# Gates of one of three dense token tiles: indirect adding DMAs into a zeroed tensor in place of one-hot matmuls

## The chip, the cores and the metric

One of the cores of a Trainium2 chip runs the whole kernel. Its engines are TensorE (PE, matrix products), VectorE (DVE), ScalarE (ACT), GpSimd (POOL) and SyncE (SP, which only starts transfers). The metric is the device time of one execution in microseconds.

## The reference

One decoder layer on 512 tokens and 16 meta tokens: projections, differential attention and a gated linear recurrence, an output projection, and then PEER, a channel mixer that chooses experts by product keys. Only PEER is touched:

```python
q = jnp.einsum('nd,dc->nc', xb, w_query).reshape(PEER_BLOCK, PEER_HEADS, 2, PEER_QUERY_DIM // 2)
s = jnp.einsum('nhpc,hpkc->nhpk', q, subkeys).astype(jnp.float32)
sv, si = lax.top_k(s, PEER_TOPK)
cand_s = (sv[:, :, 0, :, None] + sv[:, :, 1, None, :]).reshape(PEER_BLOCK, PEER_HEADS, PEER_TOPK * PEER_TOPK)
cand_i = (si[:, :, 0, :, None] * N_KEYS + si[:, :, 1, None, :]).reshape(PEER_BLOCK, PEER_HEADS, PEER_TOPK * PEER_TOPK)
top_s, pos = lax.top_k(cand_s, PEER_TOPK)
experts = jnp.take_along_axis(cand_i, pos, axis=-1).reshape(PEER_BLOCK, PEER_HEADS * PEER_TOPK)
gates = jax.nn.softmax(top_s, axis=-1).reshape(PEER_BLOCK, PEER_HEADS * PEER_TOPK)
hid = jax.nn.gelu(jnp.einsum('nkd,nd->nk', u_table[experts], xb), approximate=False) * gates
return jnp.einsum('nk,nkd->nd', hid, v_table[experts])
```

There are 128 x 128 experts of width 1024, 8 heads and 16 experts a head: each token has 128 gates. Inside a head the 16 experts differ; two heads may name the same one, and then their gates add up.

## The kernel before

The 512 tokens are four tiles of 128. For three of them (tiles 0 to 2, the dense tiles) PEER is computed over all 16,384 experts: U in 128 blocks of 128 experts against the 384 tokens (`ps_h`, 24 matmuls of 128x128 by 128x384 a block: three products per slice, since each number is split into a high and a low part), gelu into `hr`, times a dense gate matrix, then V (`y`). For the fourth tile (`SP`, number 3) the chosen rows of U and V are gathered by 256 indirect DMAs of GpSimd, 128 rows each (`ug`, `vg`).

The dense gates are a tensor in DRAM, `g_dram`, indexed by group of 32 tokens, second key, first key and token. The dense part reads it back in slices `gsl` of 4 blocks.

The stretch in question lies between the choice of the experts (about 465 us) and the dense part (from 751 us):

- `route(tb)` (L781) turns the positions in the sorted lists into expert indices, in `pick` with steps on 128x2048 elements on VectorE, each after an expansion by ScalarE (L789). For the gathered tile it ends in `exp_idx`, for a dense tile in `pmj`, transposed by TensorE (`ptp`).
- `gates4` (L832) makes the dense gates of four tokens: two VectorE operations build one-hots `oh` (L837, L843), eight TensorE matmuls (L850, L851) multiply them into `pgt`, and ScalarE copies these into `stg` (L852). After 8 calls four DMAs (L889) store 32 tokens. There are 96 calls, 32 for each dense tile.
- Between them `run_ahead` computes the hidden values of the first 40 U blocks ahead of time (the ring, `RING` = 40), in quarters of a block, `RATE` = 0.8 quarters a call of `gates4`. `h_parts` does one block: a load `ur` from SP, the high part `uh` on ScalarE, the low part `ul` on the engine that `eng` names (here GpSimd, `G`; L107), 24 matmuls and the gelu (L698).
- The dense part (L896 on) loads `gsl` (L975) and V (`vr`, L977), splits V into `vh` and `vl`, multiplies `hr` by the slice (`hr`, L982), splits that into `wh` and `wl`, and runs the `y` matmuls; `h_parts` of block i + 40 stands behind those of block i, and the gathers of the fourth tile are spread over the blocks.

A scheduler orders the instructions of each engine from the program; on VectorE in the dense part the order is that of the code. SP starts nearly all transfers, in its own order: a transfer that waits for something holds up those behind it.

In the front (the first 70 us) SP loads the weights `wr` of the projections, 512 KB each, two to a piece, and the pieces are split on ScalarE (`wh`) and VectorE (`wl`) before TensorE uses them. `mf` are masks.

Of the kernel before, what the change touches and what calls it, by code (L numbers as in the profile page):

```python
# [8 lines left out]
F32 = mybir.dt.float32  # L9
F32R = mybir.dt.float32r  # L10
F16 = mybir.dt.float16
U32 = mybir.dt.uint32
# [30 lines left out]
GI = 4  # L43
# sums of a pair of descending lists that can be among the 16 largest:
# (first row, rows, columns) of the blocks that cover (a + 1) * (b + 1) <= 16
CBLK = [(0, 1, 16), (1, 1, 8), (2, 2, 5), (4, 4, 3), (8, 8, 1)]
NCAND = sum(n * m for _, n, m in CBLK)
RING = 40
HP = 4
RATE = 0.8  # L50
DRAIN = 0.3
W2 = 10
LAG = 2


# [5 lines left out]
def tile_kernel(  # L61
# [30 lines left out]
    h_dram = dram.tile([SEQ, D], F32, name="h_dram")  # L92
    g_dram = dram.tile([DTOK // GB, NK, NK, GB], F32, name="g_dram")

# [5 lines left out]
    def rstd(dst, ssq, n, width):  # L100
        """dst = (ssq / n + eps) ** -0.5 for [P, width] tiles."""
        G.tensor_scalar(dst, ssq, 1.0 / n, EPS, op0=OP.mult, op1=OP.add)
        G.tensor_tensor(dst, dst, nhalf[: dst.shape[0], :width], op=OP.pow)
# [9 lines left out]

    # ------------------------------------------------------------------ front
    with ExitStack() as fr:
# [10 lines left out]
        with ExitStack() as pr:  # L126
# [94 lines left out]

            # ---- HGRN2 projections
            Q, QF, KR, FF = [], [], [], []
# [30 lines left out]

            # gates' lower bound: softmax over the two rows of logits, first row
            lg = fc.tile([P, 2, NH], F32, name="lg")
# [12 lines left out]
            for pc in range(2):  # L269
                for cb in range(2):  # L270
# [15 lines left out]
                    KR.append(k)  # L286
            # lambda
            lq = fc.tile([P, 4, 64], F32, name="lq")
# [22 lines left out]
            V.tensor_copy(idb, ident)  # L311

            cosr = xp.tile([P, T], F32, name="cosr")
            sinr = xp.tile([P, T], F32, name="sinr")
# [5 lines left out]
            for pc in range(2):  # L320
                w = w_piece(2 + pc)
                for cb in range(2):
# [10 lines left out]
                    QF.append(qf)  # L333
            # ---- HGRN2: scores inside the chunks, by a tree of decays
            AT = [hg.tile([P, NTB, P], F32, name=f"at{h}") for h in range(NH)]
# [43 lines left out]

            # ---- HGRN2: states at the chunks' starts and outputs  # L380
            def keys(h):
# [51 lines left out]

            # ---- attention projections
            AQ, AK = [], []
            for which, lst, lo in ((8, AQ, NMETA), (10, AK, 0)):
                for pc in range(2):
                    w = w_piece(which + pc)
                    for cb in range(2):
                        n = T - lo  # L440
                        raw = tp.tile([P, T], F32, name="raw", tag="w2", bufs=W2)
                        segs = [(lo, T)] if n <= 512 else [(0, HALF), (HALF, T)]
                        for a, b in segs:
                            ps = proj_t(w, cb, a, b)
                            S.activation(raw[:, a - lo : b - lo], ps, AF.Copy, scale=0.125 if lo else 1.0)
                        rot = tp.tile([P, T], F32, name="rot", tag="w2", bufs=W2)
                        for g in range(4):
                            src = (g ^ 1) * 32
                            nc.sync.dma_start(rot[g * 32 : g * 32 + 32, :n], raw[src : src + 32, :n])
                        hh = pc * 2 + cb  # L450
                        V.tensor_tensor(rot[:, :n], rot[:, :n], sinr[:, lo:], op=OP.mult)
                        if lo:
                            # one query of the pair per half, zeros in the other
                            r = aqp.tile([P, 2, SEQ], F32, name=f"aq{hh}")
                            G.memset(r[64:, 0], 0.0)
                            G.memset(r[:64, 1], 0.0)
                            V.tensor_tensor(raw[:, :n], raw[:, :n], cosr[:, lo:], op=OP.mult)
                            for p2 in range(2):
                                r0 = slice(p2 * 64, p2 * 64 + 64)
                                V.tensor_tensor(r[r0, p2], raw[r0, :n], rot[r0, :n], op=OP.add)  # L460
                        else:
                            r = hp_.tile([P, T], F32, name=f"ak{hh}", tag=f"f{hh}")
                            V.tensor_tensor(r, raw, cosr, op=OP.mult)
                            V.tensor_tensor(r, r, rot, op=OP.add)
                        lst.append(r)
            # ---- attention core
            def scores(h, tb):
# [61 lines left out]

            # gate of the recurrence, times the norm's weight  # L530
            wg = {}
# [112 lines left out]

        # ------------------------------------------------------ output projection
        xbp = ctx.enter_context(tc.tile_pool(name="xbp", bufs=1, reuse_waits="tile"))
# [28 lines left out]

    # --------------------------------------------------------------- PEER
    ringp = ctx.enter_context(tc.tile_pool(name="ringp", bufs=RING, reuse_waits="tile"))
# [9 lines left out]
    def h_parts(i, eng=None, n=1):  # L687
        """gelu of block i's hidden values, in n steps; the last one appends it to the ring"""
        h_load(i, eng)
        if eng is not None and i + 1 < RING:  # L690
            h_load(i + 1, eng)
# [15 lines left out]
    with ExitStack() as rt:  # L707
# [10 lines left out]
        G.iota(io_f, pattern=[[1, P]], base=0, channel_multiplier=0, allow_small_or_imprecise_dtypes=True)  # L718
        V.tensor_copy(io16, io_f[:, :16])
        starts = rc.tile([P, 16], I16, name="starts")  # L720
        o = 0
# [52 lines left out]
        rw = rt.enter_context(tc.tile_pool(name="rg", bufs=2, reuse_waits="tile"))  # L774
        steps = (None for i in range(RING) for _ in h_parts(i, G, HP))

# [4 lines left out]
        def route(tb):  # L781
            # experts' two key indices
            idx = []

            def pick(which, sel, op, key, table, dt):
                """idx of the selected key: sum over a of op(sel, key[a]) * table[a]"""
                eq = rw.tile([P, PH * TOPK, TOPK], dt, name="eq", tag="eq", bufs=1)
# [10 lines left out]

            # first list: rank a is the last one whose candidates start at or before the position;
            # 64 * key + start comes out as a sum of the table's steps  # L800
            comb = rw.tile([P, PH, TOPK], I16, name="comb", bufs=1)
# [17 lines left out]
            if tb == SP:  # L819
                V.scalar_tensor_tensor(  # L820
                    exp_idx, idx[0].rearrange("p h k -> p (h k)"), float(NK), idx[1].rearrange("p h k -> p (h k)"),
                    op0=OP.mult, op1=OP.add,
                )
                return None
            ptp = pg.tile([P, 4, P], F32, name="ptp", tag="pg")
            for i, t in enumerate((idx[0], idx[1], gh[:, tb], TS[tb])):
# [5 lines left out]
        def gates4(pmj, t0, stg, c0):  # L832
            """dense gates of four tokens: one-hots of the first key, of it times the gate's two parts, of the second"""
            oh = rw.tile([P, 4, P, 4], F16, name="oh", bufs=3)
# [19 lines left out]
        run_ahead(16)  # L854
        # gates, in two parts of 11 bits for the dense blocks
        fl = "p t h k -> p (t h) k"
# [7 lines left out]
        V.tensor_tensor(g3, g3, mx.unsqueeze(2).to_broadcast([P, NTB * PH, TOPK]), op=OP.mult)  # L864
        V.tensor_copy(exp_g, TS[SP].rearrange("p h k -> p (h k)"))
        gh16 = rw.tile([P, ND, PH, TOPK], F16, name="gh16", bufs=1)
        gh = rw.tile([P, ND, PH, TOPK], F32, name="gh", bufs=1)
# [3 lines left out]
        V.tensor_tensor(TSA[:, :ND], TSA[:, :ND], gh, op=OP.subtract)  # L871

        run_ahead(4)
        route(SP)
        run_ahead(8)
        nxt = route(0)
        run_ahead(16)
        acc_ = 0.0
        for tb in range(ND):
            pmj = nxt  # L880
            for g0 in range(0, P, GB):
# [6 lines left out]
                for i0 in range(0, NK, 32):  # L888
                    nc.sync.dma_start(g_dram[(tb * P + g0) // GB, :, i0 : i0 + 32, :], stg[:, i0 : i0 + 32, :])  # L889
                if g0 == P // 2 - GB and tb + 1 < ND:  # L890
# [5 lines left out]

    # dense part for the first ND token blocks, gathered part for the last
    with ExitStack() as dn:
# [64 lines left out]
        for i in range(NK):  # L963
# [9 lines left out]
            if i % GI == 0:  # L973
                gsl = dp.tile([P, DTOK // GB, GI, GB], F32, name="gsl", bufs=2)
                nc.sync.dma_start(gsl, g_dram[:, :, i : i + GI, :].rearrange("g j i t -> j g i t"))  # L975
            vr_ = dp.tile([P, D], F32, name="vr", tag="vr", bufs=3)
# [94 lines left out]
```

## Time and profile before

| | |
|---|---|
| Three executions | 1656.05, 1659.43, 1655.10 us |
| Median | 1656.05 us |
| Span of the profiled execution | 1655.8 us |
| TensorE busy | 1595.0 us (96%) |
| VectorE busy | 1246.4 us (75%) |
| ScalarE busy | 672.6 us (41%) |
| GpSimd busy | 566.7 us (34%) |
| Transfers | 363.93 MB, mean 220 GB/s |

The profile comes from one execution, whose span runs from its first to its last instruction and is its own time; it lies 0.25 us under the median. Busy time is the sum of an engine's instructions; TensorE's matmuls overlap, so that the duration of one (297 ns for a `pgt` matmul) is longer than the distance to the next. The chain of waits follows what ended last back through its causes. The granted clock is TensorE's, 1.00 being full speed.

### The profile page before, as it was taken

How to read it: one execution, taken by the hardware profiler on the slowest of the kernel's cores; microseconds unless marked ns; L12 is line 12 of the kernel's file. 1: busy time of each engine (PE TensorE's matmuls, PEld its weight loads, DVE VectorE, ACT ScalarE, POOL GpSimd, SP SyncE). 2: the span in 40 equal slices, each digit the busy share in tenths (PEclk: the TensorE clock that was granted, in tenths of full speed). 3: DMA queues.
4: the chain of work that ended last, by engine and by line, in shares of the span. 5: the costliest groups of instructions: out<-in, count | busy, mean ns of one | idle time of the engine just before them, and what ended most of it. 6: DMA issues, size and time to landing. Idle time of an engine off the chain costs nothing.

```text
span 1655.8 us, 23775 instructions
## 1 busy us (share of the span) xinstructions
PE 1595.0 (96%) x8859; PEld 1427.1 (86%) x8859; DVE 1246.4 (75%) x2375; ACT 672.6 (41%) x1017; POOL 566.7 (34%) x429
## 2 busy tenths in 40 slices
PE   7999998999978889999999999999999999999997
PEld 7899986888777889898999999999999999988886
DVE  6772568568898897837877778777777777767776
ACT  5123265422245666753433333333333333323333
POOL 2000012334444223254444444444444444433221
PEclk9999999999988999999999999999999999999999
DMA  6211322322222354569999988998898999877884
GB/s 205 77 50 45 118 71 103 115 90 77 73 81 100 143 203 174 207 228 357 337 322 319 324 306 308 318 323 309 311 331 304 318 321 314 311 233 262 282 278 144
DMA packets 145635, 363.93 MB, mean 220 GB/s; under 512 B 11888, under 2 KB 61296, under 8 KB 145392
## 3 DMA queue, kind: packets, MB, share of 16 engines
q1 hardware_dynamic: 107936, 227.10, 39.4%
q0 software_dynamic: 37008, 134.27, 23.4%
q8 instruction: 69, 1.13, 0.3%
q10 hardware_dynamic: 576, 1.05, 0.2%
q14 instruction: 46, 0.38, 0.1%
HBM read 330.92 MB, written 29.36 MB: 218 GB/s over the span
## 4 chain that ended last, share of the span: by engine, by line
PE 80%; DVE 13%; ACT 2%; DMA 1%; issue 1%; POOL 1%; SPq 0%; POOLq 0%; DVEq 0%; ACTq 0%
PE y L112 10%; PE y L111 10%; PE y L110 10%; PE ps_h L112 9%; PE ps_h L110 9%; PE ps_h L111 9%; PE pgt L850 2%; DVE oh L837 2%; PE pgt L851 2%; DVE oh L843 2%; PE ps_t L110 2%; PE ps_l L342 2%; PE ps_t L112 2%; PE ps_t L111 2%; PE ps_n L110 1%; PE ps_n L111 1%
## 5 line engine op out<-in xcount | busy, mean ns | idle before, releaser
L110 PE MATMUL ps_h<-xbh,uh 128*128 128x384 f32 x1024 | 355.1, 347 | 9.1 <-ACT hr L698 9.1
L112 PE MATMUL ps_h<-xbh,ul 128*128 128x384 f32 x1024 | 348.3, 340 | 3.3 <-POOL ul L107 3.3
L111 PE MATMUL ps_h<-xbl,uh 128*128 128x384 f32 x1024 | 347.6, 339 | 0.0
L110 PE MATMUL y<-vh,wh 128*128 128x512 f32 x768 | 299.0, 389 | 3.2 <-ACT wh L106 3.0
L112 PE MATMUL y<-vh,wl 128*128 128x512 f32 x768 | 300.9, 392 | 0.0
L111 PE MATMUL y<-vl,wh 128*128 128x512 f32 x768 | 300.4, 391 | 0.0
L922 POOL DMA_INDIRECT vg<-in_v_dram,exp_idx x128 | 185.3, 1448 | 277.8 <-DVE acc L928 210.6
L908 POOL DMA_INDIRECT ug<-in_u_dram,exp_idx x128 | 177.5, 1387 | 215.7 <-DVE jk L912 151.2
L107 DVE TENSOR_TENSOR vl<-vr,vh 128x1024 fp32r<-128x1024 f32 x128 | 156.8, 1225 | 123.0 <-ACT vh L106 121.1
L106 ACT ACTIVATE vh<-vr 128x1024 fp32r<-128x1024 f32 x128 | 136.0, 1062 | 266.2 <-issue 215.2
L106 ACT ACTIVATE uh<-ur 128x1024 fp32r<-128x1024 f32 x144 | 152.7, 1062 | 158.8 <-issue 69.4
L107 POOL TENSOR_TENSOR ul<-ur,uh 128x1024 fp32r<-128x1024 f32 x57 | 151.2, 2658 | 191.9 <-ACT uh L106 191.9
L110 PEld LDWEIGHTS ps_h<-xbh,uh 128*128 128x128 f32 x1024 | 197.2, 193 | 13.7 <-ACT hr L698 10.1
L111 PEld LDWEIGHTS ps_h<-xbl,uh 128*128 128x128 f32 x1024 | 196.3, 192 | 3.5
L112 PEld LDWEIGHTS ps_h<-xbh,ul 128*128 128x128 f32 x1024 | 195.3, 191 | 3.6 <-POOL ul L107 3.6
L110 PEld LDWEIGHTS y<-vh,wh 128*128 128x128 f32 x768 | 144.2, 188 | 31.9 <-ACT wh L106 4.2
L112 PEld LDWEIGHTS y<-vh,wl 128*128 128x128 f32 x768 | 144.1, 188 | 31.1 <-DVE wl L107 0.9
L111 PEld LDWEIGHTS y<-vl,wh 128*128 128x128 f32 x768 | 144.1, 188 | 28.3
L106 ACT ACTIVATE wh<-hr 128x384 fp32r<-128x384 f32 x128 | 67.2, 525 | 246.4 <-DVE hr L982 241.7
L928 DVE SCALAR_TENSOR_TENSOR acc<-vg,hid,acc 128x1024 f32<-128x1024 f32 x127 | 162.7, 1281 | 3.3 <-DMA vg<-in_v_dram,exp_idx 1.4
L912 DVE SCALAR_TENSOR_TENSOR jk<-ug,xbn 128x1024 f32<-128x1024 f32 x128 | 156.4, 1222 | 8.9 <-DMA ug<-in_u_dram,exp_idx 6.5
L107 DVE TENSOR_TENSOR wl<-hr,wh 128x384 fp32r<-128x384 f32 x128 | 71.5, 559 | 83.7 <-ACT wh L106 83.1
(268 smaller groups left out, 2716.5 us busy)
## 6 DMA issues: line engine op xcount, KB each, us to landing
ur<-in_uT_dram SPq DMA_DIRECT2D x128, 512.0 KB
vr<-in_v_dram SPq DMA_DIRECT2D x128, 512.0 KB
g_dram<-stg SPq DMA_DIRECT2D x48, 512.0 KB
gsl<-g_dram SPq DMA_DIRECT2D x32, 768.0 KB
wr<-in_w_in_dram SPq DMA_DIRECT2D x26, 512.0 KB
ur<-in_wq_dram SPq DMA_DIRECT2D x16, 512.0 KB
wor<-in_w_out_dram SPq DMA_DIRECT2D x8, 512.0 KB
xr<-in_xT_dram SPq DMA_DIRECT2D x8, 264.0 KB
```

The costliest lines, as they stand in the source:

```text
L106: S.activation(hi, src, AF.Copy)
L107: (eng or V).tensor_tensor(lo, src, hi.bitcast(F32), op=OP.subtract)
L110: PE.matmul(ps, ah, bh, start=first, stop=False)
L111: PE.matmul(ps, ah, bl, start=False, stop=False)
L112: PE.matmul(ps, al, bh, start=False, stop=last)
L342: PE.matmul(ps[:, c, :], KR[h][:, cs], rhs[:, c * P : c * P + P], start=True, stop=True)
L837: V.tensor_tensor(oh[:, :2], io128.unsqueeze(1).to_broadcast([P, 2, P, 4]), pmj[:, :2, tq4].unsqueeze(2).to_broadcast([P, 2, P, 4]), op=OP ...
L843: V.tensor_tensor(oh[:, 2:], oh[:, 0:1].to_broadcast([P, 2, P, 4]), pmj[:, 2:, tq4].unsqueeze(2).to_broadcast([P, 2, P, 4]), op=OP.mult,)
L908: G.indirect_dma_start(out=ug, out_offset=None, in_=u, in_offset=bass.IndirectOffsetOnAxis(ap=exp_idx[:, k : k + 1], axis=0))
L912: V.scalar_tensor_tensor(jk, ug, 1.0, xbn_, op0=OP.mult, op1=OP.mult, accum_out=hid[:, k : k + 1])
L922: G.indirect_dma_start(out=vg, out_offset=None, in_=v, in_offset=bass.IndirectOffsetOnAxis(ap=exp_idx[:, k : k + 1], axis=0))
L928: V.scalar_tensor_tensor(acc, vg, hid[:, k : k + 1], acc, op0=OP.mult, op1=OP.add)
```

## The change

Tile 0's gates are no longer made by `gates4`. A tile `zero` is cleared by GpSimd in the front, and SP writes it over the whole of `g_dram[0]` in four transfers of 2 MB. When `route(0)` has the indices, two VectorE operations compute the place of each gate in `g_dram[0]`, `sc_idx`, from the two keys, the group and the token (`base_i`). `scatter` then issues 128 indirect DMAs from GpSimd, one for each head and rank; each adds 128 gates of 4 bytes, one per token, into `g_dram[0]`. The DMAs of one head are independent of each other; each DMA of a head waits for all 16 of the head before.

`g_dram` becomes three tensors, one per dense tile, and the load of a slice three transfers; the first of them waits for the last head. The loop over `gates4` runs over tiles 1 and 2 only, with `RATE` 1.5. The routes come in the order 0, `SP`, 1 (then 2 inside the loop) where they came in the order `SP`, 0 (then 1 and 2). The low parts `ul` of the look-ahead blocks are made by VectorE.

```diff
-RATE = 0.8
+RATE = 1.5
...
-    g_dram = dram.tile([DTOK // GB, NK, NK, GB], F32, name="g_dram")
+    g_dram = [dram.tile([P // GB, NK, NK, GB], F32, name=f"g_dram{t}") for t in range(ND)]
...
+            zero = tp.tile([P, 16, GB], F32, name="zero", tag="w2", bufs=W2)
+            G.memset(zero, 0.0)
+            for g in range(P // GB):
+                nc.sync.dma_start(
+                    g_dram[0][g].rearrange("j (a b) t -> j a b t", b=16),
+                    zero.unsqueeze(1).to_broadcast([P, NK // 16, 16, GB]),
+                )
...
-        if eng is not None and i + 1 < RING:
+        if n > 1 and i + 1 < RING:
             h_load(i + 1, eng)
...
+        base_i = rc.tile([P, 1], F32, name="base_i")
+        for g in range(P // GB):
+            G.iota(
+                base_i[g * GB : g * GB + GB], pattern=[[0, 1]], base=g * NK * NK * GB, channel_multiplier=1,
+                allow_small_or_imprecise_dtypes=True,
+            )
...
-        steps = (None for i in range(RING) for _ in h_parts(i, G, HP))
+        steps = (None for i in range(RING) for _ in h_parts(i, None, HP))
...
+            if tb == 0:
+                off = rc.tile([P, PH, TOPK], F32, name="off")
+                sc_idx = rc.tile([P, PH, TOPK], U32, name="sc_idx")
+                V.tensor_scalar(off, idx[0], float(GB), base_i[:, 0:1], op0=OP.mult, op1=OP.add)
+                V.scalar_tensor_tensor(sc_idx, idx[1], float(NK * GB), off, op0=OP.mult, op1=OP.add)
+                return sc_idx
...
+        sc_g = rc.tile([P, PH, TOPK], F32, name="sc_g")
+        V.tensor_scalar(sc_g, TS[0], GS, None, op0=OP.mult)
...
+        def scatter(sc_idx):
+
+            flat = g_dram[0].rearrange("g j i t -> (g j i t)").unsqueeze(1)
+            before = []
+            for h in range(PH):
+                now = []
+                for k in range(TOPK):
+                    ins = G.indirect_dma_start(
+                        out=flat, out_offset=bass.IndirectOffsetOnAxis(ap=sc_idx[:, h, k : k + 1], axis=0),
+                        in_=sc_g[:, h, k : k + 1], in_offset=None, compute_op=OP.add,
+                    ).ins
+                    tc.declare_no_dep(ins, group=f"head{h}", reason="one head's experts differ")
+                    tc.add_to_no_dep_group(f"head{h}", ins)
+                    for b in before:
+                        tc.add_manual_dep(ins, b.name, SYNC, reason="the head before may have the same expert")
+                    now.append(ins)
+                before = now
+            return before
+
         run_ahead(4)
+        scattered = scatter(route(0))
+        run_ahead(8)
         route(SP)
         run_ahead(8)
-        nxt = route(0)
+        nxt = route(1)
         run_ahead(16)
         acc_ = 0.0
-        for tb in range(ND):
+        for tb in range(1, ND):
...
-                    nc.sync.dma_start(g_dram[(tb * P + g0) // GB, :, i0 : i0 + 32, :], stg[:, i0 : i0 + 32, :])
+                    nc.sync.dma_start(g_dram[tb][g0 // GB, :, i0 : i0 + 32, :], stg[:, i0 : i0 + 32, :])
...
-                nc.sync.dma_start(gsl, g_dram[:, :, i : i + GI, :].rearrange("g j i t -> j g i t"))
+                for t in range(ND):
+                    gs_ = nc.sync.dma_start(
+                        gsl[:, t * (P // GB) : (t + 1) * (P // GB)],
+                        g_dram[t][:, :, i : i + GI, :].rearrange("g j i t -> j g i t"),
+                    ).ins
+                    if t == 0:
+                        for b in scattered:
+                            tc.add_manual_dep(gs_, b.name, SYNC, reason="the last head's gates")
```

GpSimd's order behind the candidates' sums (`cand`), before: 35 low parts, then the gathers `ug`.

```order
L763 TENSOR_TENSOR cand<-sva 128x4x10
L763 TENSOR_TENSOR cand<-sva 128x4x12
L763 TENSOR_TENSOR cand<-sva 128x4x8
L763 TENSOR_TENSOR cand<-sva 128x4x16
L107 TENSOR_TENSOR ul<-ur,uh 128x1024 x35
L908 DMA ug<-in_u_dram,exp_idx 128x1024 x2
```

And now: the 128 scatters stand there, and one low part is left (of the block behind the ring); the gathers come behind them.

```order
L779 TENSOR_TENSOR cand<-sva 128x4x12
L779 TENSOR_TENSOR cand<-sva 128x4x8
L779 TENSOR_TENSOR cand<-sva 128x4x16
L904 DMA g_dram_61<-sc_g,sc_idx 2097152x1 x128
L108 TENSOR_TENSOR ul<-ur,uh 128x1024
L953 DMA ug<-in_u_dram,exp_idx 128x1024 x32
```

The low parts have left GpSimd, and the scatter stands between the sums and the fourth tile's gathers.

SP's order at the start of the dense part, before (`g_dram<-stg` the gates' stores, `ur` U blocks, `gsl` the first slice, `vr` V blocks):

```order
L889 DMA g_dram<-stg 128x1024 x4
L655 DMA ur<-in_uT_dram 128x1024 x2
L889 DMA g_dram<-stg 128x1024 x4
L655 DMA ur<-in_uT_dram 128x1024 x2
L975 DMA gsl<-g_dram 128x12x128
L977 DMA vr<-in_v_dram 128x1024 x3
L655 DMA ur<-in_uT_dram 128x1024
L977 DMA vr<-in_v_dram 128x1024
```

And now:

```order
L934 DMA g_dram_63<-stg 128x1024 x4
L664 DMA ur<-in_uT_dram 128x1024 x3
L934 DMA g_dram_63<-stg 128x1024 x4
L1021 DMA gsl<-g_dram_61 128x4x128
L1021 DMA gsl<-g_dram_62 128x4x128
L1021 DMA gsl<-g_dram_63 128x4x128
L1029 DMA vr<-in_v_dram 128x1024 x3
```

The slice is three transfers, of which that from `g_dram_61` (tile 0's) waits for the scatter; the first three V blocks follow behind it, as before.

VectorE's order ahead of the first one-hot `oh`, before (`eq`, `sif`, `ix` are steps of `route(0)`; the last `eq`, `starts` is the first of `route(1)`):

```order
L790 TENSOR_TENSOR eq<-eq,io_3431 128x2048
L792 TENSOR_TENSOR eq<-eq,sif 128x2048
L794 TENSOR_TENSOR eq<-eq 128x128x8
L817 CAST sif<-si_3456 128x128
L794 TENSOR_TENSOR eq<-eq 128x128x4
L794 TENSOR_TENSOR eq<-eq 128x128x2
L796 TENSOR_TENSOR ix_5046<-eq 128x128
L790 TENSOR_TENSOR eq<-eq,starts 128x2048
L837 TENSOR_TENSOR oh<-io_3432,pmj 128x1024 x2
L843 TENSOR_TENSOR oh<-oh,pmj 128x1024 x2
L837 TENSOR_TENSOR oh<-io_3432,pmj 128x1024
```

And now (steps of `route(1)`, the third one, and then the first of `route(2)`):

```order
L108 TENSOR_TENSOR ul<-ur,uh 128x1024
L806 TENSOR_TENSOR eq<-eq,io_3439 128x2048
L808 TENSOR_TENSOR eq<-eq,sif 128x2048
L108 TENSOR_TENSOR ul<-ur,uh 128x1024
L810 TENSOR_TENSOR eq<-eq 128x128x8
L833 CAST sif<-si_3470 128x128
L810 TENSOR_TENSOR eq<-eq 128x128x4
L810 TENSOR_TENSOR eq<-eq 128x128x2
L812 TENSOR_TENSOR ix_5291<-eq 128x128
L806 TENSOR_TENSOR eq<-eq,starts 128x2048
L859 TENSOR_TENSOR oh<-io_3440,pmj 128x1024 x2
L865 TENSOR_TENSOR oh<-oh,pmj 128x1024 x2
```

The first one-hot stands behind a third route, and low parts `ul` stand between the routes' steps: 18 of them ahead of the first one-hot, where there were none. TensorE has 409 `ps_h` matmuls ahead of the first `pgt` matmul where it had 264, and 986 ahead of the first `y` matmul where it had 960.

## Rows read from the trace of the kernel before

**Rows 1.** Windows, all engines: busy us (count); then granted clock, DMA share, GB/s.

```profile
core 0: us, PE busy (x) PEld busy (x) DVE busy (x) ACT busy (x) POOL busy (x), PEclk, DMA share, GB/s
...
680.00:737.00 57.00, 56.23 (x380) 52.43 (x380) 36.59 (x45) 35.90 (x40) 20.14 (x9) 1.00 0.58 213
737.00:751.00 14.00, 11.35 (x66) 11.02 (x64) 1.69 (x2) 3.86 (x6) 7.41 (x5) 1.00 1.01 386
751.00:800.00 49.00, 48.62 (x244) 43.97 (x245) 42.84 (x63) 19.14 (x28) 24.61 (x17) 1.00 0.96 348
800.00:900.00 100.00, 100.00 (x508) 91.08 (x507) 80.05 (x99) 36.43 (x49) 45.30 (x34) 1.00 0.91 321
```

**Rows 2.** Chain of waits, 720 to 760: start, length, what.

```profile
737.37 13.41 DMA vr<-in_v_dram
...
751.38 0.50 PE y L110
```

**Rows 3.** Timeline of SP's queue: start, length, line, transfer.

```profile
41.95 54.72 SPq L141 DMA_DIRECT2D wr<-in_w_in_dram  x8
...
735.62 0.38 SPq L975 DMA_DIRECT2D gsl<-g_dram  x1
```

**Rows 4.** Timeline of VectorE in the routes: start, length; idle before, who ended it.

```profile
470.81 3.28 DVE L792 TENSOR_TENSOR eq<-eq,step 128x2048 int16<-128x2048 int16 x1
...
482.91 1.22 DVE L792 TENSOR_TENSOR eq<-eq,sif 128x2048 f16<-128x2048 f16 x1
...
491.21 0.29 DVE L820 SCALAR_TENSOR_TENSOR exp_idx<-ixa,ix 128x128 uint32<-128x128 f32 x1
...
508.96 0.43 DVE L796 TENSOR_TENSOR ix<-eq 128x128 f32<-128x128 f16 x1
...
513.04 1.28 DVE L837 TENSOR_TENSOR oh<-io,pmj 128x1024 f16<-128x1024 f16 x2
```

**Rows 5.** Timeline of TensorE, 468 to 482; 18 matmuls from 470.90 to 476.75.

```profile
470.90 0.69 PE L110 MATMUL ps_h<-xbh,uh 128*128 128x384 f32 x1 [5.34 <-ACT hr L698]
471.38 0.53 PE L111 MATMUL ps_h<-xbl,uh 128*128 128x384 f32 x1
471.70 0.53 PE L112 MATMUL ps_h<-xbh,ul 128*128 128x384 f32 x1
...
476.75 0.33 PE L110 MATMUL ps_h<-xbh,uh 128*128 128x384 f32 x1
476.92 0.34 PE L111 MATMUL ps_h<-xbl,uh 128*128 128x384 f32 x1
```

**Rows 6.** Windows of `pgt` alone: TensorE, ScalarE busy; then clock, DMA.

```profile
680.00:725.00 45.00, 25.76 (x192) 26.13 (x24) 1.00 0.54 198
```

**Rows 7.** Windows of `ps_h` alone: TensorE, its weight loads, ScalarE.

```profile
725.00:740.00 15.00, 15.00 (x88) 15.00 (x87) 1.42 (x3) 1.00 0.80 280
```

**Rows 8.** Tile `oh`: durations in ns as min/median/max.

```profile
L837 DVE TENSOR_TENSOR oh<-io,pmj x96: 673/686/2823, 513.0 to 719.1; 128x1024 f16<-128x1024 f16 x96
```

**Rows 9.** Line 107 (low parts): min/median/max ns.

```profile
L107 DVE TENSOR_TENSOR ul<-ur,uh x87: 1210/1218/1221, 758.3 to 1466.0; 128x1024 fp32r<-128x1024 f32 x87
...
L107 POOL TENSOR_TENSOR ul<-ur,uh x57: 2343/2412/5164, 312.8 to 742.5; 128x1024 fp32r<-128x1024 f32 x57
```

**Rows 10.** Timeline of GpSimd, gathers of 735 to 775 and from 1500.

```profile
740.28 0.95 POOL L908 DMA_INDIRECT ug<-in_u_dram,exp_idx  x1 [0.16 <-issue]
741.54 0.94 POOL L908 DMA_INDIRECT ug<-in_u_dram,exp_idx  x1 [0.30 <-issue]
...
1500.80 1.74 POOL L922 DMA_INDIRECT vg<-in_v_dram,exp_idx  x1 [2.34 <-DVE acc L928]
```

**Rows 11.** Timeline of VectorE at 1500.

```profile
1500.49 1.23 DVE L107 TENSOR_TENSOR vl<-vr,vh 128x1024 fp32r<-128x1024 f32 x1
```

**Rows 12.** Line 908, the gathers of U: min/median/max ns.

```profile
L908 POOL DMA_INDIRECT ug<-in_u_dram,exp_idx x128: 934/1516/1865, 735.3 to 1440.4; - x128
```

**Rows 13.** Tile `rot`: idle time before its users (us, times), by releaser.

```profile
  DMA rot<-raw: 17.0, 8
```

**Rows 14.** Timeline of ScalarE in the front.

```profile
48.00 2.01 ACT L106 ACTIVATE wh<-wr 128x1024 fp32r<-128x1024 f32 x2 [4.02 <-PE ps_t L111]
```

**Rows 15.** Timeline of TensorE in the front.

```profile
63.61 0.36 PE L110 MATMUL ps_n<-wh,xh 128*128 128x256 f32 x1
```

More of the change, by code (lines that the diff above doesn't have):

```diff
@@ L53 @@
 LAG = 2
+SYNC = mybir.DependencyInfo(mybir.DependencyClass.Sync, mybir.DependencyReason.DATA)
 def row_bcast(ap, n, parts=P):
```

## The prediction, made before the changed kernel ran

> **What bounds the kernel now.** I read the windows table first. TensorE is full nearly everywhere; from 680 on it is the longest bar in every stretch but one [rows 1]. That one, 737 to 751, is the seam this change works on: the last gates are stored, TensorE runs out of look-ahead blocks, and the dense part has not begun. The chain of waits says why [rows 2]: the first y matmul at 751.38 waits for a V block that was 13.41 us on its way, asked for by SP only after the gates' first slice, `gsl`, at 735.62 [rows 3]: 15.8 us from slice to first y. So whatever lets SP issue that slice earlier moves everything after it, until TensorE is what is late. After the seam TensorE has no slack (100.00 of 100 us, 800 to 900 [rows 1]), so a time gained or lost at the first y arrives at the end undiminished. That is the frame of the sum: when does the first y start, and how much look-ahead is then already done.
>
> Ahead of the gates the bound is another: VectorE turns sums into expert indices (route), and its first one-hot starts at 513.04 [rows 4], while TensorE stands still in parts and runs at the lower of its two clock levels, half pace (1.2 for 2.4 GHz): after a wait of 5.34 us at 470.90 the matmuls come 0.32 us apart, from 476.92 on 0.18 [rows 5]. From 517 to the seam the gates' work is a mix: three TensorE jobs (look-ahead, gates, a few transposes) one behind the other.
>
> **What leaves TensorE.** Tile 0's 32 groups of gates go: 256 `pgt` matmuls. In a stretch with 192 of them TensorE counted 25.76 us [rows 6], 134 ns each, so 34 us leave. The look-ahead stays: 88 `ps_h` matmuls took 15.00 us [rows 7], 0.170 each. The VectorE one-hots (64 of 0.68 us [rows 8]), copies and stores of that tile go too; they lie beside TensorE's work and I count them at nothing.
>
> **What moves on VectorE before the first one-hot.** Three routes now precede it (tile 0, the gathered tile, tile 1) where two did. One route takes from the end of the gathered tile's (491.21) to the end of tile 0's (508.96), 17.8 us [rows 4]; without the two steps that were held up beside GpSimd, 14. Eighteen `ul` parts come to VectorE ahead of the first one-hot at 1.22 us each [rows 9]: +22. Against that GpSimd's `ul` work vanishes, and with it the collisions: the same multiplication took 3.28 us beside it and 1.22 alone [rows 4]; six such steps lie in 467 to 513, 2.1 each: -12.5. Sum: 513.0 + 14 + 22 - 12.5 = 536.5; the first gate matmul some 4 us behind, as before: 540.5. In that time TensorE can run 409 look-ahead matmuls where it had 264 (the program's order), 25 us more in 24 us more, so its stand-still there stays as it was.
>
> **When TensorE is ready for the dense part.** From 540.5: 577 look-ahead matmuls (986 less 409) at 0.170 = 98, and 64 groups of 8 gate matmuls at 0.134 = 69; 707.5. The same count for before (696 and 768 from 517.1) gives 738, and the last look-ahead ended about 748 (11.35 of 14 us busy [rows 1]); half of that slack, since two thirds of the groups are left and nothing slows the one-hots: 712. VectorE's load there (128 one-hots at 0.68, 22 `ul` at 1.22, one route) is 130 us of 170, so it does not bind.
>
> **When the scatter ends.** This is the new wait, and the largest unknown. SP's first `gsl` waits for the eighth head; in the order SP has V's loads behind that wait, so V's split and the first y wait with it. The indices: before, the first route ended at 491.21 [rows 4]; now four collisions less (-8.4), ten `ul` on VectorE up to there (+12.2): 495. Then eight heads one behind the other, each 15 issues and the last one's flight. No row shows an accumulating indirect DMA; the nearest are the gathers, which GpSimd issues the same way. Free, one starts 1.26 us after the last (740.28 to 741.54); one that meets a VectorE operation with two inputs in SBUF waits until it ends: 1.74 at 1500.80 beside a subtraction that ran from 1500.49 [rows 10, 11]. The median over the dense part is 1.52 [rows 12], which with 0.30 between makes 1.82. In the scatter's time VectorE is busy some three quarters with operations of 0.68 and 1.22 us, so that an issue waits 0.75 x 0.42 = 0.32: 1.58, between the ends 1.26 and 1.82. The flight: small rope transfers held VectorE up 17.0 us in 8 times, 2.1 each [rows 13], a floor; the ceiling is the 13.41 us of rows 2, in a crowd that the scatter doesn't have. I take 4.5, twice the floor, since an addition reads before it writes; that is a choice. A head: 15 x 1.58 + 4.5 = 28.2; eight: 226; the end at 721. Ends: 1.26 and 2.1 give 663, 1.82 and 8 give 778.
>
> On the issue cost the Trainium skill speaks otherwise ("SBUF — State Buffer", Who interferes with whom): a tensor_tensor takes only the shared pair's read side, and descriptor generation is inferred to need the write side, so the two should pass each other. Rows 10 and 11 show a subtraction of just that kind with a gather behind it; I go by the row. By the rule the issues would stay at 1.26 (first rival). On the flight it speaks against the change ("DMA: Bandwidth & Descriptors", Anatomy of one DMA): a fixed cost of about 2.0 us, mostly the receipt of the write, heaviest in HBM; no row shows it for 4-byte additions. By 2.0 the head would be 25.7 and the scatter's end 701.
>
> **The first y.** With 721 as the later of the two (TensorE 712), SP then issues three slices and V. Before it took 15.8 us with a look-ahead U block and four 512 KB gathers in the queue at 386 GB/s [rows 1]; now the U block is there already, and less is ahead of V: I take 11, bounds 8 and 16. The first y at 732 against 751.4: -19.4. TensorE stood 20 us, so some 18 matmuls run at half pace [rows 5]: +2.6. By then 26 look-ahead matmuls more are done than before (986 against 960): -4.4.
>
> **The front.** GpSimd clears a tile, SP sends four 2 MB zero writes ahead of the weights that it issues at 41.95 [rows 3]. At 386 GB/s 8.4 MB take 22 us, from about 32 to 54, at 300 to 60. The two weight splits at 48.00 [rows 14] would then find their data at 55 to 62, and TensorE wants them at 63.61 [rows 15]; a split and its low part are 2 to 3.5 us. So 0 to 4 us: I take 2, and up to 9 if the transfers behind it pile up.
>
> **Sum:** 1655.8 - 19.4 + 2.6 - 4.4 + 2 = 1636.6; the profiled span lies 0.25 under the median of 1656.05, so about 1637.
>
> **Rivals.** (A) The scatter is not late. If a head takes under 25.8 us (issues at 1.26 to 1.4), it ends by 701 and TensorE alone sets the first y, at 713: -38.4 - 4.4 + 2 = 1615. At the free pace of rows 10 a head is 15 x 1.26 + 4.5 = 23.4 and the end 682. For it: most of VectorE's gate work is of short operations, and no row shows one of 0.68 us holding an issue up. Against: the 1.8 us of rows 10 and 12. The Trainium skill's rule on the shared pair, above, would bring just this case. 0.25. (B) The scatter is slower than what it replaces. GpSimd's issues behind VectorE, or additions with a long flight: a head over 30.6 us puts the end past 740 and the first y past 751, and from there each us per head costs eight. At the dense part's 1.82 and 4.5 a head is 31.8, the end 749, the first y 760, and 1655.8 + 8.8 + 2.6 + 2 - 4.4 = 1665; with a flight of 8, 35.3, 777 and 1692. For it: the median of rows 12 and 128 issues that can't overlap across heads; nothing in the trace bounds an addition's flight. 0.30 beyond +0.3%. (C) The zeroing stops the front: 9 us in place of 2 makes 1644, inside the range. (D) The freed TensorE time is not on the path because VectorE's longer preamble eats it: if the first gate came at 560, TensorE would be ready at 732, still with the scatter; it would change nothing by itself.
>
> **How the numbers follow.** Chances: the forecast's mechanism (a scatter that ends between 701 and 736, time 1615 to 1651) 0.35; A 0.25; about even (end 736 to 746; within 0.3%, which is what a measurement of this kernel can tell from none) 0.10; B 0.30. Faster 0.60, same 0.10, slower 0.30. The range leaves out a tenth on each side: 1612 (A without a front delay) to 1690 (B with a flight of 8). Without B the likeliest one's own range is 1615 to 1651.
>
> **What would show it.** Starts of the first scatter (495), of each head (28 apart) and of the last; the wait on SP before the first `gsl`, and who ends it; first one-hot at 536; TensorE's idle time ahead of the first y, some 20 us; the first y near 732; the half-pace matmuls behind it; the weight split of 48.00 at 55 to 62. The forecast is wrong if a head takes under 25 or over 31 us, or if TensorE, not SP, is the last to arrive.

## The result and the profile after

The changed kernel takes 1692.4 us (median of 4 runs, 1689.8 to 1697.0) against 1655.6 of the kernel before: 1.0225 times as long, with a 95% interval of 1.0205 to 1.0246. Forecast were 1637 us, and a range of 1612 to 1690. The profiled execution spans 1695.2 us. From its page (the third line is TensorE's granted clock in 40 slices, the last the queue of GpSimd's transfers):

```profile
span 1695.2 us, 23411 instructions
...
PE 1559.5 (92%) x8599; PEld 1397.2 (82%) x8599; DVE 1197.9 (71%) x2354; ACT 642.1 (38%) x984; POOL 683.7 (40%) x522
...
PEclk9999999999899999656999999999999999999999
...
q0 software_dynamic: 55440, 134.34, 25.4%
```

In slices 17 to 19 the granted clock falls to 0.5 and 0.6. The windows around them (columns as in [rows 1]):

```profile
640.00:680.00 40.00, 40.00 (x271) 37.32 (x270) 28.34 (x38) 25.02 (x29) 28.64 (x18) 1.00 0.66 185
680.00:692.00 12.00, 11.27 (x73) 10.43 (x71) 0.10 (x1) 6.92 (x9) 10.17 (x7) 1.00 0.24 2
692.00:770.00 78.00, 0.00 (x0) 0.00 (x0) 0.00 (x0) 0.22 (x1) 61.72 (x41) 0.51 0.20 0
770.00:790.00 20.00, 7.25 (x24) 6.93 (x24) 1.70 (x2) 3.37 (x4) 7.16 (x6) 0.59 0.82 289
790.00:800.00 10.00, 9.62 (x30) 7.71 (x31) 8.68 (x14) 2.41 (x4) 4.34 (x3) 0.67 1.05 404
800.00:900.00 100.00, 100.00 (x507) 90.89 (x505) 84.80 (x117) 36.68 (x51) 49.38 (x35) 1.00 0.95 340
```

TensorE is through with all that it may do at 691 and does nothing until 773; in 692 to 770 only GpSimd works (and ScalarE for 0.22 us). The y matmuls start at 790.38, where they started at 751.38 [rows 2]: 39.0 us later, and the span is 39.4 us longer. SP's queue (start, length), then TensorE's timeline:

```profile
670.16 103.46 SPq L664 DMA_DIRECT2D ur<-in_uT_dram  x3
773.68 3.63 SPq L934 DMA_DIRECT2D g_dram<-stg  x4
777.69 2.94 SPq L1021 DMA_DIRECT2D gsl<-g_dram  x3
780.68 1.61 SPq L1029 DMA_DIRECT2D vr<-in_v_dram  x3
```

```profile
773.33 0.69 PE L113 MATMUL ps_h<-xbh,ul 128*128 128x384 f32 x1 [82.06 <-POOL ul L108]
...
790.38 0.79 PE L111 MATMUL y<-vh,wh 128*128 128x512 f32 x1 [9.80 <-ACT wh L107]
790.97 0.63 PE L112 MATMUL y<-vl,wh 128*128 128x512 f32 x1
791.40 0.63 PE L113 MATMUL y<-vh,wl 128*128 128x512 f32 x1
...
796.78 0.39 PE L111 MATMUL y<-vh,wh 128*128 128x512 f32 x1
797.01 0.40 PE L112 MATMUL y<-vl,wh 128*128 128x512 f32 x1
```

Two waits stand there at once. SP's first slice goes out at 777.69, against 735.62 [rows 3]. And TensorE's own wait of 82.06 us is put down to GpSimd's `ul`: the low part of block 40, which stands behind the 128 scatters on GpSimd. The profile alone doesn't say which of the two is the cost. After the wait the y matmuls come 0.43 apart, which is the lower clock level as in [rows 5]; from 796.78 on they come 0.23 apart.

The scatter itself, GpSimd's timeline: the first issue, then starts of heads (604.81, 638.94, 709.07, 741.54) and last issues of heads (634.56, 736.86, 769.35):

```profile
490.60 1.74 POOL L904 DMA_INDIRECT g_dram<-sc_g,sc_idx  x1 [26.50 <-DVE sc_idx L845]
...
604.81 1.55 POOL L904 DMA_INDIRECT g_dram<-sc_g,sc_idx  x1 [2.44 <-DMA g_dram<-sc_g,sc_idx]
606.66 2.40 POOL L904 DMA_INDIRECT g_dram<-sc_g,sc_idx  x1 [0.30 <-issue]
...
615.29 1.55 POOL L904 DMA_INDIRECT g_dram<-sc_g,sc_idx  x1 [0.30 <-issue]
...
634.56 1.83 POOL L904 DMA_INDIRECT g_dram<-sc_g,sc_idx  x1 [0.30 <-issue]
638.94 1.54 POOL L904 DMA_INDIRECT g_dram<-sc_g,sc_idx  x1 [2.55 <-DMA g_dram<-sc_g,sc_idx]
...
709.07 1.54 POOL L904 DMA_INDIRECT g_dram<-sc_g,sc_idx  x1 [1.59 <-DMA g_dram<-sc_g,sc_idx]
...
736.86 1.55 POOL L904 DMA_INDIRECT g_dram<-sc_g,sc_idx  x1 [0.30 <-issue]
741.54 1.54 POOL L904 DMA_INDIRECT g_dram<-sc_g,sc_idx  x1 [3.13 <-issue]
...
769.35 1.55 POOL L904 DMA_INDIRECT g_dram<-sc_g,sc_idx  x1 [0.30 <-issue]
```

All 128, min/median/max in ns:

```profile
L904 POOL DMA_INDIRECT g_dram<-sc_g,sc_idx x128: 1539/1551/6097, 490.6 to 769.3; - x128
```

### The profile page after: what moved, and what is told of

Same layout as the page of the kernel before. It is cut to its first block, busy times and chain, and to the rows that moved or that the text cites. A ratio compares the mean times of both kernels' runs of the same rounds, so it can differ in the third digit from the quotient of the medians.

```text
span 1695.2 us, 23411 instructions
## 1 busy us (share of the span) xinstructions
PE 1559.5 (92%) x8599; PEld 1397.2 (82%) x8599; DVE 1197.9 (71%) x2354; ACT 642.1 (38%) x984; POOL 683.7 (40%) x522
## 3 DMA queue, kind: packets, MB, share of 16 engines
q0 software_dynamic: 55440, 134.34, 25.4%
## 4 chain that ended last, share of the span: by engine, by line
PE 70%; POOL 13%; DVE 7%; issue 4%; DMA 3%; ACT 2%; SPq 1%; POOLq 0%; DVEq 0%; ACTq 0%
POOL g_dram L904 12%; PE y L112 10%; PE y L113 10%; PE y L111 10%; PE ps_h L113 7%; PE ps_h L111 7%; PE ps_h L112 7%; DMA g_dram<-sc_g,sc_idx 2%; PE ps_l L351 2%; PE ps_t L113 2%; PE ps_t L111 2%; PE ps_t L112 2%; PE ps_n L111 1%; PE ps_n L112 1%; PE ps_n L113 1%
## 5 line engine op out<-in xcount | busy, mean ns | idle before, releaser
L111 PE MATMUL ps_h<-xbh,uh 128*128 128x384 f32 x1024 | 350.2, 342 | 1.3 <-ACT hr L707 1.3
L904 POOL DMA_INDIRECT g_dram<-sc_g,sc_idx x128 | 222.4, 1737 | 84.4 <-issue 38.8
L108 DVE TENSOR_TENSOR ul<-ur,uh 128x1024 fp32r<-128x1024 f32 x127 | 155.0, 1221 | 7.9 <-ACT uh L107 7.8
```

The costliest lines, as they stand in the source:

```text
L108: (eng or V).tensor_tensor(lo, src, hi.bitcast(F32), op=OP.subtract)
L111: PE.matmul(ps, ah, bh, start=first, stop=False)
L904: ins = G.indirect_dma_start(out=flat, out_offset=bass.IndirectOffsetOnAxis(ap=sc_idx[:, h, k : k + 1], axis=0), in_=sc_g[:, h, k : k + 1] ...
```

## The experiments

Each comparison has its own runs of the kernel before on the same chip: 1655.6 for the changed kernel; 1659.2 for no scatter, four heads, last low part on VectorE and plain writes; 1658.7 for two targets, before with low parts on VectorE, and the two partial tiles; 1658.2 (one run) for plain writes, paced. Ratios stand with their 95% intervals; a kernel without one ran once.

| kernel | us | ratio to before | last scatter issued | first y |
|---|---|---|---|---|
| changed kernel | 1692.4 | 1.0225 [1.0205, 1.0246] | 769.4 | 790.4 |
| no scatter | 1608.2 | 0.9691 [0.9674, 0.9707] | - | 704.5 |
| four heads | 1611.5 | 0.9709 [0.9693, 0.9725] | 632.0 | 704.9 |
| last low part on VectorE | 1688.5 | 1.0173 [1.0156, 1.0190] | 764.8 | 782.7 |
| two targets | 1680.3 | one run | 757.0 | 774.7 |
| plain writes | 1732.8 | one run | 670.2 | 827.6 |
| plain writes, paced | 1658.9 | one run | 732.4 | 752.7 |
| before, low parts on VectorE | 1633.9 | 0.9847 [0.9831, 0.9864] | - | 730.4 |
| three quarters of the tile | 1642.2 | 0.9897 [0.9880, 0.9913] | 719.2 | 738.6 |
| half of the tile | 1619.5 | 0.9765 [0.9748, 0.9781] | 658.3 | 711.7 |

### Is it the scatter that is waited for?

No scatter at all:

```diff
-            for h in range(PH):
+            for h in range(0):
                 now = []
```

> Leaves out all 128 adding DMAs (tile 0's gates stay zero in the output); the zeroing, the indices and the moved low parts stay. If the scatter is what TensorE waits for (it stood from 691 to 773 in the changed kernel), the first y comes when the 986 look-ahead matmuls are through, near 695 to 700, with no half-pace stretch: 790 - 697 = 93 us less, about 1600 us. If the freed TensorE time were not on the path, because VectorE's longer preamble eats it, the time stays above 1640.

Measured: 1608.2 us, first y at 704.5. The rest of the change is worth 51 us; the scatter costs some 84 by the times and 88 by the ratios. The freed TensorE time is on the path.

Half of the heads (`range(PH // 2)` at the same place):

> Leaves out heads 4 to 7 of the scatter (their gates are missing for tile 0). 64 issues at 1.85 to 2.3 from 490: the last head ends near 635, ahead of TensorE's 691. Theory scatter: nothing is left to wait for, the same as with no scatter at all, about 1600 us. If GpSimd's issues also hurt VectorE or TensorE while they run, it stays above that by what they cost, 5 us or more.

Measured: 1611.5, first y at 704.9, the last issue at 632.0. A scatter that ends before TensorE costs 3.3 us, no more.

### Which of the two waits?

```diff
         for i in range(RING, RING + 1):
-            h_load(i, G)
+            h_load(i, None)
```

> Only the low part of block 40, which stands behind the scatter on GpSimd and for which TensorE waited 82 us, goes to VectorE. Theory scatter: the first slice still waits for the last head (about 774); SP's stores no longer hang behind the U load, so the slice comes 3 to 4 us earlier and the time is 1686 to 1692. Rival, the low part is the wait: TensorE goes on and the time falls to 1600 to 1620.

Measured: 1688.5. What TensorE now waits for ahead of y (us in total, times, longest), and ScalarE's wait behind it; then SP's stores of the last gates and its first slice:

```profile
PE y L111 <- ACT wh L107: 88.7, 2, 88.3
ACT vh L107 <- DMA vr<-in_v_dram: 84.5, 2, 84.3
```

```profile
687.01 2.87 SPq L934 DMA_DIRECT2D g_dram<-stg  x4
767.89 1.48 SPq L1021 DMA_DIRECT2D gsl<-g_dram  x3
```

TensorE waited 82 us for the low part and now waits 88 for the first y's operand. The named wait was a cover: it went, and the one behind it took its place. What it was worth is small: 3.9 us by the times, 8.6 by the ratios (1.0173 for 1.0225). In the changed kernel a U load had to wait for the buffer that GpSimd's low part held, so that SP's stores of the last gates went out at 773.68 only and the slice behind them at 777.69, 8.3 behind the last issue. Here the stores went at 687.01 and the slice at 767.89, 3.1 behind the last issue. So SP's queue is 5.3 of the 7.7 us by which the first y comes earlier in the two profiled executions; 4.5 are a scatter that ended earlier, for a reason that stays open, and 2.1 were lost again between slice and first y.

### What makes a head long: issue or flight?

Heads alternate between two zeroed tensors and wait for the head before the last; block 40's low part is on VectorE, as in the kernel above:

```diff
-            flat = g_dram[0].rearrange("g j i t -> (g j i t)").unsqueeze(1)
-            before = []
+            flats = [x.rearrange("g j i t -> (g j i t)").unsqueeze(1) for x in (g_dram[0], g_alt)]
+            befores = [[], []]
             for h in range(PH):
+                flat, before = flats[h % 2], befores[h % 2]
...
-                before = now
-            return before
+                befores[h % 2] = now
+            return befores[0] + befores[1]
```

> Heads alternate between two zeroed tensors (the second is never read, so tile 0 lacks the gates of heads 1, 3, 5, 7), and a head waits for the one before the last; block 40's low part is on VectorE. Theory: the pace of the issues makes most of a head, its flight the rest; the gap from the last issue to the next head falls from about 4 us to 1.85, seven times 2.2 = 15 us earlier than with block 40's low part alone (1688): 1670 to 1677. If the flights were the larger part, 1640 or less.

Measured: 1680.3, one run: 8 us off where some 15 were expected. The step from a head's last issue to the next head fell from 4.4 on the mean of seven (in the kernel above) to 2.2, the expected 15 in all; but the first scatter started 3.2 us later, in a kernel with twice the zeroing in its front, and the 120 steps inside the heads took 4.0 more. Flights are the small part: 31 us in the seven steps above, against 244 in the 120.

Writes in place of additions:

```diff
-                        in_=sc_g[:, h, k : k + 1], in_offset=None, compute_op=OP.add,
+                        in_=sc_g[:, h, k : k + 1], in_offset=None,
```

> The 128 indirect DMAs write instead of adding (an expert that two heads name gets one gate only). If it is the addition that makes an issue take 1.55 us where the gathers took 0.95, issues fall to 0.95 + 0.30 = 1.25, a head to about 23, the last head ends near 680 and the time is about 1600 us. If the 1.55 belongs to the direction or to the 4-byte elements, nothing changes: 1690 us, issues of 1.55.

Measured: the issue fell as the first theory says, and the time did the opposite of what I expected, 1732.8. All 128 issues, then windows:

```profile
L904 POOL DMA_INDIRECT g_dram<-sc_g,sc_idx x128: 952/958/2312, 489.5 to 670.2; - x128
```

```profile
560.00:600.00 40.00, 4.68 (x27) 4.18 (x28) 5.02 (x7) 4.53 (x5) 28.91 (x30) 0.50 0.12 41
...
611.00:642.00 31.00, 0.69 (x5) 0.45 (x5) 2.52 (x4) 2.09 (x2) 22.59 (x24) 0.50 0.02 0
...
700.00:750.00 50.00, 50.00 (x341) 46.64 (x339) 36.71 (x50) 32.23 (x36) 0.00 (x0) 1.00 0.49 171
```

The median issue is 0.958 us, where the addition has 1.551, and the last one goes out at 670.2 instead of 769.4. So the addition itself costs GpSimd 0.59 us an issue. But from about 530 to 671 nearly all else stood: in the first and second of these windows TensorE was busy 4.68 of 40 and 0.69 of 31 us, and the transfers moved 41 and 0 GB/s. Its time is therefore no measure of the issue; the durations are.

The same writes with a small copy on GpSimd between any two:

```diff
+                    cp = G.tensor_copy(pace[:, h], sc_idx[:, h, :]).ins
+                    for b in before:
+                        tc.add_manual_dep(cp, b.name, SYNC, reason="pace")
```

> As the plain writes (an expert that two heads name gets one gate only), but GpSimd copies a small tile between any two of them, so that they go out about as far apart as the additions did (1.8 to 2.1 us in place of 1.26). If it was the pace of 128 four-byte writes each 1.26 us that starved every other transfer and the engines' instructions from 530 to 671, the starving is gone or much weaker: the scatter ends near 740 to 760 and the time is 1660 to 1690, TensorE's work done by 700. If it belongs to plain four-byte writes at any pace, TensorE still stands from 530 on until the last of them: 1760 or more.

Measured: 1658.9, one run. The issue stays at 0.984 us, the last one goes out at 732.4, and TensorE and the transfers (last column) work through the same stretch:

```profile
560.00:600.00 40.00, 40.00 (x265) 37.73 (x264) 32.38 (x50) 26.14 (x29) 32.66 (x37) 1.00 0.61 211
```

A scatter that ends 37 us earlier than the changed kernel's brings the first y 37.7 us earlier (752.7 for 790.4): TensorE waited for it there too. So four-byte writes alone, at this slower pace, bring no standstill.

### One part alone, and less of the scatter

The kernel before with the look-ahead's low parts on VectorE, block 40's too (the first line keeps the early load of the next block):

```diff
-        if eng is not None and i + 1 < RING:
+        if n > 1 and i + 1 < RING:
...
-        steps = (None for i in range(RING) for _ in h_parts(i, G, HP))
+        steps = (None for i in range(RING) for _ in h_parts(i, None, HP))
...
-            h_load(i, G)
+            h_load(i, None)
```

> The kernel before with one part of the change alone: the low parts of the look-ahead on VectorE, no scatter. Theory: the collisions of VectorE with GpSimd (12 us ahead of the first one-hot, and the one-hots that took 2.5 to 2.9 us) go, 22 us of subtractions come; TensorE stays the bound from 517 on: 1643 to 1655. Rival, the subtractions delay the first one-hot and it arrives at the end: 1660 or more.

Measured: 1633.9, 25 us faster than before, beyond the theory's range. Windows of it, and then of the kernel before, the second of each up to just ahead of its seam:

```profile
460.00:513.00 53.00, 47.70 (x258) 47.06 (x259) 45.22 (x124) 26.92 (x29) 2.10 (x5) 0.91 0.38 120
513.00:720.00 207.00, 201.71 (x1382) 187.38 (x1381) 164.07 (x252) 142.94 (x152) 0.42 (x1) 0.98 0.51 185
```

```profile
460.00:513.00 53.00, 37.43 (x182) 35.94 (x181) 45.78 (x115) 22.73 (x23) 22.77 (x13) 0.81 0.21 70
513.00:737.00 224.00, 212.36 (x1433) 196.09 (x1432) 181.46 (x227) 145.21 (x157) 78.48 (x29) 0.98 0.49 177
```

Ahead of 513 TensorE works 47.70 us where it worked 37.43; behind it, it is busy 97% of the time instead of 95%. Its one-hots (ns, min/median/max) no longer have a long one; the longest was 2823 [rows 8]:

```profile
L837 DVE TENSOR_TENSOR oh<-io,pmj x96: 677/684/696, 512.7 to 703.5; 128x1024 f16<-128x1024 f16 x96
```

The first one-hot comes at 512.7 where it came at 513.0 [rows 4]: VectorE is busy 45.22 us ahead of it, where it was 45.78, so the subtractions that came to it and the collisions that left it balance.

Half of the tile by scatter (tokens 0 to 63, the ranks of a head packed in pairs), the other half by one-hots. Block 40's low part is on VectorE, `RATE` is 1.15, and only this half is zeroed. From its edit:

```diff
-            for g0 in range(0, P, GB):
+            for g0 in range(0 if tb else 64, P, GB):
...
+                    V.scalar_tensor_tensor(
+                        dst, idx[1][:64, :, ks], float(NK * GB), off[:64, :, ks], op0=OP.mult, op1=OP.add
+                    )
+                G.dma_start(sc_idx[64:], sc_hi)
...
-                for k in range(TOPK):
+                for k in range(8):
```

> Only tokens 0 to 63 of tile 0 are scattered, two ranks of a head packed into one DMA: 64 DMAs, 8 to a head; tokens 64 to 127 go through the one-hots again (16 groups), and the low part of block 40 is on VectorE. Theory scatter: 7 x 2.0 + 4 a head, 8 heads, ends near 640, ahead of TensorE; TensorE has 16 groups more than without the scatter (1608), 17 us: 1620 to 1628, faster than both kernels. Rival, GpSimd's issues cost the others time whatever their number: above 1640.

Measured: 1619.5, faster than both kernels, at 0.9765 of before. The last scatter, and the windows of the end of the gates, with TensorE full up to 680:

```profile
658.30 1.70 POOL L912 DMA_INDIRECT g_dram<-sc_g,sc_idx  x1 [0.30 <-issue]
```

```profile
640.00:680.00 40.00, 40.00 (x279) 36.99 (x278) 31.23 (x44) 27.21 (x30) 14.07 (x8) 1.00 0.60 189
680.00:720.00 40.00, 36.11 (x206) 32.59 (x205) 18.61 (x26) 20.01 (x25) 8.01 (x7) 0.96 0.82 300
```

Three quarters (96 tokens, 12 DMAs a head, `RATE` 1.3):

> Tokens 0 to 95 scattered with 96 DMAs, 12 to a head (8 with two ranks for tokens 0 to 63, 4 with four ranks for tokens 64 to 95), the last 32 tokens by one-hots. Theory scatter: 11 x 2.0 + 4 a head, ends near 705, level with TensorE (691 + 8): first y near 716, 1616 to 1628. If a head takes what it took in the changed kernel per issue (2.2 with flight), 96 end at 701; if issues are slower, each us comes out eightfold.

Measured: 1642.2, outside the range. The last issue goes out at 719.23, not near 705, and TensorE waits:

```profile
719.23 1.54 POOL L928 DMA_INDIRECT g_dram<-sc_gq,sc_idq  x1 [0.31 <-issue]
```

```profile
PE y L112 <- ACT wh L108: 38.2, 1, 38.2
```

The steps between heads were 5.9 us on the mean of seven, for the 4 that I had put in. By these two the balance lies between 64 and 96 DMAs.

## Why the prediction was wrong

The picture of the seam held: the first y sets the end, the last head sets the slice, and rival B (the scatter is later than what it replaces) is what happened. The term that failed is the scatter's.

**The pitch of the issues: the failed step.** It was built on "Free, one starts 1.26 us after the last", from a gather in [rows 10]. A free addition starts 1.85 after the last: from 709.07 to 736.86 are 15 steps, 27.79 us, with VectorE silent and transfers at 0 GB/s. That floor already lies above the upper end of 1.82 which the prediction took from [rows 12]; plain writes, 0.958 an issue like the gathers, show that it is the addition. The second part, waiting for VectorE, was put at 0.32 and was about right: 604.81 to 634.56 are 29.75 us in 15 steps, 1.98, or 0.13 over the floor, and the mean over 62 steps of 528 to 680 is 2.12, 0.27 over it; over all 120 steps inside heads it is 0.19. The form of the wait was right too. The issue at 606.66 took 2.40, 0.85 over the free 1.55; VectorE's subtraction ended 0.98 after it began:

```profile
606.42 1.22 DVE L108 TENSOR_TENSOR ul<-ur,uh 128x1024 fp32r<-128x1024 f32 x1
```

The issue at 615.29, where VectorE had just ended a one-hot, took 1.55. Of the 55 issues that began with more than 0.14 us of a VectorE operation left, 40 were longer than 1.55 by what was left less 0.13, within 0.02. The Trainium skill ("SBUF — State Buffer", Who interferes with whom) infers that a tensor_tensor lets descriptor generation pass; the trace disagrees, by 0.85 us at 606.66.

Over the whole scatter, 769.35 - 490.60 = 278.75 us, seven of the steps lead to a next head and take 33.7 together; the other 120 take 245.1, 2.04 each. Against 1.58 that is 120 x 0.46 = 55 us. All the rest nearly cancels: start 490.6 instead of 495 (-4.4), flights 4.8 instead of 4.5 (+2). The end is 721 + 55 + 2 - 4 = 774, and 769.35 and a flight give the same. An estimate from these rows: with the 0.59 us of the addition gone from each of the 120 steps, 71 us in all, the last issue would stand near 698, level with TensorE's 695 below. No run shows that, since the writes at their own pace stopped the rest.

**The flight** was put at 4.5 as a choice, from a floor of 2.1 [rows 13]: measured 4.8, with 3.1 to 4.7 in the quiet stretch. Of these the issue itself is 1.55; the wait behind it was 1.59 ahead of 709.07 and 3.13 ahead of 741.54. The fixed cost of about 2.0 us that the Trainium skill gives ("DMA: Bandwidth & Descriptors", Anatomy of one DMA) lies between the two. Not all of the 3.13 is the transfer. The chain of waits has the last DMA of that head on its way for 2.94 from the start of its issue, 1.4 from its end, and for the 1.74 behind it the profile names no release:

```profile
736.86 2.94 DMA g_dram<-sc_g,sc_idx
739.80 1.74 issue
```

**When TensorE is ready:** forecast 712, measured 691 and the 24 look-ahead matmuls that had to wait (22 of them block 40's), at 0.173 each: 695 in all. Two steps were wrong. The first one-hot came at 529.3, not 536.5. And the stand-still ahead of it did not stay as it was: the low parts on VectorE alone let TensorE do 10 us more ahead of 513 (47.70 for 37.43), and in the changed kernel it does 50.34:

```profile
460.00:513.00 53.00, 50.34 (x274) 50.34 (x275) 45.53 (x120) 27.92 (x30) 21.76 (x15) 0.92 0.41 120
```

Put at a cost of 9.5 us there, that part is worth 25 us by itself. It is the likely reason why the rest of the change came out better than forecast (1608.2 without the scatter, where rival A had 1615); no run separates it there. So the scatter had less time, not more, to hide in.

**The first y** comes 12.7 us after the slice (777.69 to 790.38), put at 11; the slice goes 3.6 us behind the 774 above, and 5.3 later behind the last issue than with block 40's low part on VectorE, because of SP's queue. That a U load holds SP up, I had not followed: I counted its low part as moved with the others, though the order shows it behind the scatter.

**The clock:** 2.6 us forecast; the 15 matmuls from 790.38 to 796.78 took 6.4 us, and at 0.23 each would have taken 3.4: 3.0. **The 26 matmuls ahead**, -4.4, stand as they were.

**The front:** 2 us forecast, none found. The zero writes went out from 31.08 and filled the queue at 385 GB/s; the weights behind them were there in time:

```profile
31.08 12.30 SPq L317 DMA_DIRECT2D g_dram<-zero  x4
43.49 50.97 SPq L142 DMA_DIRECT2D wr<-in_w_in_dram  x8
```

```profile
31.00:44.00 13.00, 12.37 (x71) 10.61 (x70) 11.77 (x24) 5.23 (x7) 1.66 (x3) 1.00 1.02 385
...
62.00:70.00 8.00, 8.00 (x72) 8.00 (x72) 6.88 (x14) 1.67 (x2) 0.00 (x0) 1.00 0.03 7
```

In 62 to 70 TensorE is full. The same stretch of the kernel before had the product of [rows 15] at 63.61; now it starts at 61.7. Rival C falls. With twice the zeroing the first query product (`ps_q`), at 333.2 in the changed kernel and 334.8 in the one before, came at 336.8 in its one run, so little room may be left for a second tensor.

**Sum:** 39.0 at the first y, +3.0 for the clock, -4.4 is 37.6 of the 39.4 that the spans differ; 1.8 is not accounted for. Rival B's own end, 1692, has the measured time, but from a pitch of 1.82 and a flight of 8, where 2.04 and 4.8 were found: that the two agree is luck.

## What to carry to other kernels

Where an operation that the trace doesn't have is issued 128 times in a chain, the price of one is the forecast, and a relative's price is not to be taken for it: 0.59 us an issue is, by the estimate above, 71 us over the chain, and the change lost 37 in all. Measure that one operation first, or move only as much of the work as ends before the engine that it is to relieve: half of the scatter is faster than all of it (1619.5 against 1692.4), and faster than none (1633.9 with the low parts moved, at the `RATE` of before). And take a change apart: its small part, the low parts' move to another engine, gave 25 us alone, and the long wait that the trace named (82 us) was worth 4 to 9.

## What was not expected of the hardware

An indirect DMA that adds 4-byte elements holds GpSimd 1.55 us, one that writes them 0.96. The additions went out as 144 packets a DMA and the writes as 32, by the packets of that queue over those of the gathers alone (55440, 41104 and 37008, over 128).

While 128 DMAs of 128 four-byte writes each went out, most of them 1.26 us apart, nearly everything else stopped for some 140 us: transfers stood, and instructions of TensorE came up to 2.8 us apart with no wait that the profile names:

```profile
661.85 0.48 PE L113 MATMUL ps_h<-xbh,ul 128*128 128x384 f32 x1 [2.31 <-issue]
664.65 0.48 PE L111 MATMUL ps_h<-xbh,uh 128*128 128x384 f32 x1 [2.32 <-issue]
```

With a copy of 0.22 us (the median) between them this was gone; they were then 1.35 apart when VectorE was idle and 1.8 to 2.0 when it wasn't. Each of the two kernels ran once. What is held up in the first case, and whether the pace or the copy decides, stays open.
